# The gate product of layer 0 by seven half-width products

## The chip, the cores and the metric

The kernel runs on one core of a Trainium2 chip. The metric is the device time of one execution in microseconds (us). The core has five engines with instruction streams of their own: PE (matrix products, with weight loads listed apart as PEld), DVE and ACT (elementwise work), POOL and SP, which here mostly issue transfers. Sixteen DMA engines move the data of all queues.

## The reference

Two layers act on 256 tokens x and 256 context tokens, each with 2048 features. Every layer normalises, scales and shifts its input by a modulation computed from a condition vector, widens it to 4096 features, and projects it back. Layer 0 is a Fourier branch, layer 1 is attention with a window, context keys and a sink. The change is in layer 0:

```
u, z = split(h @ w_in, 2)            # h: 2048 features, u and z: 4096
f = real(fft2(u in 16 groups)) mixed per group by w_mix
y = f * silu(z)                      # the gate
x = x + gate * (y @ w_out)
```

The same is done with the context tokens, which have their own modulation but share the weights. So z is one product of 2048 x 4096 weights with 512 columns: 256 tokens and 256 context tokens. The modulation of layer 1 and the gate of layer 0 are products of a vector with 2048 x 2048 matrices (`adw`).

## The kernel before, in words

All products are made in parts: a value is split into a high part (`h`, rounded to fp32r by ACT, L60) and a low part (`l`, the rest, by DVE, L61), and `mm3` (L73 to L75) adds high x high, high x low and low x high in PSUM. `half_split` does that for half a raw weight tile (128 x 1024) into a pool of six buffers, that is three pairs; `raw` loads a 1 MB weight tile on SP's queue into one of three buffers.

The stages, in order of time on the page: the modulation of layer 0 and a transform along the tokens (to 120 us); the spectral stage, which computes f group by group (120 to 330 us) with matmuls of 256 and 260 columns and stores f to device memory (`fd`, L514); the gate stage (330 to 690 us, L558 to L618); the output product of layer 0 in two sweeps of 16 steps (to about 1030 us, L643 to L665); the key and value projection of layer 1 (`wkv`, to about 1123 us, L733 to L744), with the rope of the keys after it (L755); attention with the query and gate projections of layer 1 between its steps; the last output product.

In the spectral stage `fold_uh` makes sums and differences of weight halves. Some sums are made by a transfer on POOL's queue that adds its source to the tile it writes (L133, 508 bytes per run).

The gate stage first makes the 16 modulated input tiles `hs` (`make_hs`, L566: two operations on DVE and one on ACT per half, the input brought by POOL's queue). Each tile has 256 token columns and 256 context columns, as a high and a low part; together they fill 32 of the 34 buffers of the pool `act`. Four blocks of 128 output features are computed together while the inputs arrive, and then 28 blocks one by one: two weight halves are split, 16 x 3 matmuls of 512 columns run, `z_out` (L580) applies silu on ACT and multiplies by f on DVE (L584). f waits in 32 resident tiles `y`, loaded from `fd` by SP.

The generator `ada_jobs` (L530) does the remaining modulation as side work for DVE: 64 jobs, each a 1 MB weight tile and eight dot products of 512 columns (L545; the last 16 jobs four). One job is taken per block of the gate stage, 36 in the output stage by `ada_rate`. In the output stage the resident `y` are split again in each of the two sweeps (`y_split0`, L624).

The order of instructions on each engine comes from a scheduler that runs at build time: it takes program order as priority and what it simulates as ready. `tc.issue_after` adds an edge that holds the order by hand. Buffers of a pool are reused when all readers are done.

Of the kernel before, what the change touches and what calls it, by code (L numbers as in the profile page):

```python
# [10 lines left out]
F32 = mybir.dt.float32  # L11
F32R = mybir.dt.float32r
# [4 lines left out]
P = 128  # L17
# [4 lines left out]
N = 256  # L22
# [6 lines left out]
def tile_dit(ctx: ExitStack, tc: tile.TileContext, a: dict, out: bass.AP):  # L29
# [13 lines left out]
    def raw(src, q=None):  # L43
        t = rawp.tile([P, D], F32, tag="raw", name="raw")
        n = src.shape[-1]
        last_dma[0] = (q or nc.sync).dma_start(t[:, :n], src).ins
        return t

# [101 lines left out]
    r_bc = adap.tile([P, 512], F32, name="r_bc")  # L150

# [281 lines left out]


# [86 lines left out]
    def ada_done(i):  # L521
        layer, which, dst = ((0, 2, gt0), (1, 1, gs1), (1, 0, sh1), (1, 2, gt1))[i]
        ns = dst.shape[-1]
        V.tensor_tensor(acc[:, i, 0:2, :, 0:ns], acc[:, i, 0:2, :, 0:ns], acc[:, i, 2:4, :, 0:ns], op=ALU.add)
        V.tensor_tensor(dst, acc[:, i, 0, :, 0:ns], acc[:, i, 1, :, 0:ns], op=ALU.add)
        V.tensor_tensor(dst, dst, adab[:, layer, which, :, 0:ns], op=ALU.add)
        if (layer, which) == (1, 1):
            V.scalar_tensor_tensor(dst, dst, 1.0, ng[:, 1], op0=ALU.add, op1=ALU.mult)

    def ada_jobs():  # L530
        for pieces in ((0,), (1, 2, 3)):
            for kh in range(2):
                cb = adap.tile([P, 2, 1024], F32, tag="cb", name="cb")
                with tc.issue_after(hs_end[2]):
                    nc.gpsimd.dma_start(cb, a["crow"][:, kh].broadcast_to([P, 2, 1024]))
                with tc.issue_after(hs_end[1]):
                    S.activation(cb, cb, AF.Silu)  # L537
                for i in pieces:
                    for fg in range(8):
                        w = raw(a["adw"][i, kh, fg])  # L540
                        for f in range(2):
                            for kq in range(2):
                                wf = w[:, f * 1024 + kq * 512 : f * 1024 + kq * 512 + 512]
                                for s in range(2 if i < 3 else 1):
                                    V.tensor_tensor_reduce(junk if s == 0 and i < 3 else wf, wf, cb[:, s, kq * 512 : kq * 512 + 512], 1.0, 0.0, ALU.mult, ALU.add, acc[:, i, kh * 2 + kq, fg * 2 + f, s : s + 1])  # L545
# [11 lines left out]
    acc = adat.tile([P, 4, 4, KT, 2], F32, name="acc")  # L557
    with tc.tile_pool(name="yp", reuse_waits="tile", bufs=32) as ypool:  # L558
        ys = []
        for b in range(NB):  # L560
            y = ypool.tile([P, 512], F32, tag="y", name="y")
            ys.append(y)
        hs = []
        hs_end = [None] * 3

        def make_hs(k):  # L566
            xt = act()
# [9 lines left out]
            hs.append((h, l))  # L577

        with tc.tile_pool(name="zp", reuse_waits="tile", bufs=2) as zp:
            def z_out(b, o):  # L580
                y = ys[b]
                z = zp.tile([P, 512], F32, tag="z", name="z")
                S.activation(z, o, AF.Silu)
                V.tensor_tensor(y, y, z, op=ALU.mult)  # L584
                if b >= 4:
                    with tc.issue_after(hs_end[0]) if b < 8 else nullcontext():
                        next(ada)

            o4 = [psum() for _ in range(4)]
            for kg in range(4):  # L590
                wr = raw(a["wz0"][kg])
                w = []
                for i in range(2):
                    make_hs(kg * 4 + i * 2)
                    with tc.issue_after(hs_end[0]) if kg else nullcontext(), tc.issue_after(hs_end[1]) if kg else nullcontext():
                        w.append(half_split(wr, i))
                    make_hs(kg * 4 + i * 2 + 1)
                for j in range(4):
                    k = kg * 4 + j
                    wh, wl = w[j // 2]  # L600
                    for b in range(4):
                        q = slice((j % 2) * 512 + b * P, (j % 2) * 512 + (b + 1) * P)
                        mm3(o4[b], wh[:, q], wl[:, q], hs[k][0], hs[k][1], k == 0, k == KT - 1)
            for b in range(4):
                with tc.issue_after(last_dma[0]):
                    nc.sync.dma_start(ys[b], fd[b])
            for b in range(4):
                z_out(b, o4[b])
            for b in range(4, NB):
                w = ws_split(raw(a["wz"][b - 4]))  # L610
                with tc.issue_after(last_dma[0]):
                    nc.sync.dma_start(ys[b], fd[b])
                o = psum()
                for k in range(KT):
                    wh, wl = w[k // 8]
                    q = slice((k % 8) * P, (k % 8 + 1) * P)
                    mm3(o, wh[:, q], wl[:, q], hs[k][0], hs[k][1], k == 0, k == KT - 1)
                z_out(b, o)  # L618


        x1, sqs = [], []
        yy = {}

        def y_split0(i):  # L624
            for j in range(2):
                h, l = act(F32R), act(F32R)
                split(h, l, ys[i % 16 * 2 + j])
                yy[i, j] = (h, l)

# [14 lines left out]
        ada_rate = {2: 2, 5: 2, 8: 2, 11: 2, 15: 0, 16: 0, 19: 2, 22: 2, 25: 2, 28: 2, 30: 0, 31: 0}  # L644
        y_split0(0)
        for i in range(32):
# [4 lines left out]
            if i < 31:  # L651
                y_split0(i + 1)
            if kg >= 12:
# [12 lines left out]


# [11 lines left out]
    o = psum()  # L679
    PE.transpose(o[0:KT, 0:P], gt1.rearrange("p k s -> p (k s)"), ident)  # L680
    gr = const.tile([KT, P], F32, name="gr")
    S.copy(gr, o[0:KT, 0:P])
    nc.gpsimd.dma_start(gated.rearrange("o (k p) -> (o k) p", p=P), gr)
# [32 lines left out]
    with tc.tile_pool(name="h1", reuse_waits="tile", bufs=16) as h1p:  # L716
# [3 lines left out]
        with tc.tile_pool(name="kvp", reuse_waits="tile", bufs=2) as kvp:  # L720
            hc1 = []
# [12 lines left out]
            for kg in range(8):  # L734
                w = ws_split(raw(a["wkv"][kg]))
                for j in range(2):
                    k = kg * 2 + j
                    wh, wl = w[j]
                    for tb in range(4):
                        h = (hx1, hc1)[tb // 2][k]  # L740
                        c = (tb % 2) * P
                        for kv in range(2):
                            q = slice(kv * 512, (kv + 1) * 512)
                            mm3(o[tb][kv], h[:, c : c + P], h[:, N + c : N + c + P], wh[:, q], wl[:, q], k == 0, k == KT - 1)  # L744
            kr = []
            for tb in range(4):
# [6 lines left out]
                t = kvp.tile([P, 512], F32, tag="kr", name="kr", bufs=4)  # L753
# [5 lines left out]
            for hp in range(4):  # L759
# [5 lines left out]
                kT.append(t)  # L765

# [444 lines left out]
```

## Time and profile before

| | |
|---|---|
| median of three runs | 1863.13 us (1860.94 to 1863.33) |
| the profiled execution | 1861.45 us |
| its span in the trace | 1859.1 us |
| granted TensorE clock, mean | 0.995 |
| gate stage, 380 to 690 us | DVE 242.0 us busy of 310, DMA share 0.59, 219 GB/s |
| transfers in all | 367 MB, 198 GB/s |

A row of a group has: line, engine, operation, what it writes and reads, shape, number | busy time in all, mean duration of one in ns | idle time of that engine before it and what ended the wait. Rows of stretches give busy time of PE, weight loads, DVE, ACT and POOL with the number of instructions, then the granted clock, the share of the DMA engines in use, and GB/s. A matmul's duration is longer than the distance of two starts, because matmuls are pipelined; the pace is read from the starts.

### The profile page before, as it was taken

What the parts mean: (1) busy time and instruction counts of PE and PEld (TensorE: products, weight loads), DVE (VectorE), ACT (ScalarE), POOL (GpSimd) and SP (SyncE); (2) the same over time, 40 slices, a digit from 0 to 9 for tenths busy, and PEclk for the clock granted to TensorE, in tenths of its full rate; (3) what the DMA queues carried; (4) which work ended last, traced back from release to release, by engine and by line L of the source; (5) the groups of instructions that cost most, each with busy time, mean ns of one, the idle gap of its engine ahead of it and who ended that gap; (6) DMA issues with size and microseconds to landing.
All of it is one profiled execution on the core that took longest, in us unless ns stands there. A gap on an engine that the chain in (4) does not pass through costs nothing.

```text
span 1859.1 us, 26469 instructions
## 1 busy us (share of the span) xinstructions
PE 1817.6 (98%) x9889; PEld 1549.3 (83%) x9889; DVE 1389.6 (75%) x2766; ACT 954.6 (51%) x1657; POOL 176.8 (10%) x189
## 2 busy tenths in 40 slices
PE   6899999999999999999999999999999999999997
PEld 4579999888888888888888787888888888887886
DVE  4669888786868788687974825888878878887455
ACT  5444444432222243224322624888888888896343
POOL 0011111100000000000000001111220220300001
PEclk9899999999999999999999999999999999999999
DMA  9999888666656647763675323333333333434543
GB/s 395 407 296 246 246 220 242 228 226 244 224 212 234 227 172 264 264 236 131 226 286 204 114 92 143 128 136 126 124 115 135 136 115 135 159 137 179 186 178 136
DMA packets 76127, 367.39 MB, mean 198 GB/s; under 512 B 23200, under 2 KB 23344, under 8 KB 40928
## 3 DMA queue, kind: packets, MB, share of 16 engines
q1 hardware_dynamic: 49104, 324.83, 47.3%
q0 software_dynamic: 22320, 33.15, 7.1%
q10 hardware_dynamic: 4576, 7.74, 1.3%
q8 instruction: 77, 1.26, 0.3%
q14 instruction: 50, 0.41, 0.1%
HBM read 353.10 MB, written 12.59 MB: 197 GB/s over the span
## 4 chain that ended last, share of the span: by engine, by line
PE 90%; DMA 4%; DVE 3%; ACT 2%; issue 1%; POOL 0%; ACTq 0%; POOLq 0%; SPq 0%; DVEq 0%
PE ps L74 23%; PE ps L73 23%; PE ps L75 23%; PE ps L910 6%; PE ps L912 3%; DMA raw<-in_awp 3%; PE ps L966 3%; PE ps L981 2%; PE ps L980 2%; PE ps L946 2%; PE ps L947 2%; DMA raw<-in_wu 1%; PE ps L208 1%; PE ps L829 0%; DVE wl L61 0%
## 5 line engine op out<-in xcount | busy, mean ns | idle before, releaser
L60 ACT CAST wh<-raw 128x1024 fp32r<-128x1024 f32 x333 | 349.5, 1051 | 556.3 <-PE ps L74 483.5
L61 DVE TENSOR_TENSOR wl<-raw,wh 128x1024 fp32r<-128x1024 f32 x333 | 421.7, 1269 | 263.0 <-ACT wh L60 260.6
L74 PE MATMUL ps<-act,wh 128*128 128x512 f32 x1024 | 398.2, 389 | 0.0
L73 PE MATMUL ps<-act,wh 128*128 128x512 f32 x1024 | 393.6, 389 | 0.0
L75 PE MATMUL ps<-act,wl 128*128 128x512 f32 x1024 | 391.2, 389 | 0.0
L75 PEld LDWEIGHTS ps<-act,wl 128*128 128x128 f32 x1024 | 192.2, 188 | 39.9
L74 PEld LDWEIGHTS ps<-act,wh 128*128 128x128 f32 x1024 | 192.2, 188 | 39.8
L73 PEld LDWEIGHTS ps<-act,wh 128*128 128x128 f32 x1024 | 192.2, 188 | 39.8
L910 PE MATMUL ps<-h,wh 128*128 128x512 f32 x512 | 186.7, 400 | 0.0
L545 DVE CUSTOM_DVE_ANT_0 raw<-raw,cb 128x512 f32<-128x512 f32 x256 | 172.8, 689 | 14.5 <-DMA raw<-in_adw 10.6
L545 DVE CUSTOM_DVE_ANT_0 junk<-raw,cb 128x512 f32<-128x512 f32 x192 | 132.0, 687 | 10.8 <-ACT cb L537 8.3
L912 PE MATMUL ps<-h,wl 128*128 128x256 f32 x512 | 138.1, 280 | 0.0
L74 PE MATMUL ps<-wl,h 128*128 128x512 f32 x320 | 125.6, 392 | 1.5 <-DVE wl L61 1.5
L73 PE MATMUL ps<-wh,h 128*128 128x512 f32 x320 | 124.3, 397 | 0.2 <-ACT h L729 0.2
L75 PE MATMUL ps<-wh,h 128*128 128x512 f32 x320 | 124.4, 391 | 0.0
L910 PEld LDWEIGHTS ps<-h,wh 128*128 128x128 f32 x512 | 96.1, 188 | 18.7
L948 DVE CUSTOM_DVE_ANT_0 ps<-ps,mask,nsink 128x512 f32<-128x512 f32 x128 | 92.1, 754 | 11.8 <-PE ps L947 10.8
L951 ACT ACTIVATE p<-ps,mx 128x512 f32<-128x512 f32 x128 | 87.3, 687 | 24.6 <-DVE mx L948 24.0
L912 PEld LDWEIGHTS ps<-h,wl 128*128 128x128 f32 x512 | 96.8, 189 | 1.4
L61 DVE TENSOR_TENSOR pl<-ps,ph 128x512 fp32r<-128x512 f32 x128 | 83.7, 685 | 9.9 <-ACT ph L60 8.9
L956 ACT ACTIVATE p<-p,sm 128x512 f32<-128x512 f32 x128 | 85.4, 716 | 7.8 <-DVE sm L954 7.8
L74 PE MATMUL ps<-wl,ys 128*128 128x512 f32 x212 | 83.3, 393 | 0.0
(311 smaller groups left out, 3572.7 us busy)
## 6 DMA issues: line engine op xcount, KB each, us to landing
raw<-in_wz SPq DMA_DIRECT2D x64, 1024.0 KB, 4.9
raw<-in_adw SPq DMA_DIRECT2D x64, 1024.0 KB, 4.9
raw<-in_awp SPq DMA_DIRECT2D x32, 1024.0 KB, 13.8
raw<-in_wo SPq DMA_DIRECT2D x32, 1024.0 KB, 5.9
raw<-in_wq SPq DMA_DIRECT2D x32, 1024.0 KB, 4.8
raw<-in_wu SPq DMA_DIRECT2D x32, 1016.0 KB, 7.3
raw<-in_wo1b SPq DMA_DIRECT2D x16, 1024.0 KB, 4.9
act<-in_xT POOLq DMA_DIRECT2D x32, 256.0 KB, 5.6
```

The lines of the kernel that those rows point to most:

```text
L60: S.copy(h, src)
L61: V.tensor_tensor(l, src, h.bitcast(F32), op=ALU.subtract)
L73: PE.matmul(o, wh, xh, start=start, stop=False)
L74: PE.matmul(o, wh, xl, start=False, stop=False)
L75: return PE.matmul(o, wl, xh, start=False, stop=stop).ins
L545: V.tensor_tensor_reduce(junk if s == 0 and i < 3 else wf, wf, cb[:, s, kq * 512 : kq * 512 + 512], 1.0, 0.0, ALU.mult, ALU.add, acc[:, i, ...
L910: PE.matmul(o[0], wh[:, q], hx1[k], start=k == 0, stop=k == KT - 1)
L912: PE.matmul(o[0][:, 0:N], wl[:, q], hx1[k][:, 0:N], start=False, stop=False)
L948: V.tensor_tensor_reduce(o, o, mask[:, tb, :], -0.125, nsink[:, i : i + 1], ALU.add, ALU.min, mx[:, tb : tb + 1])
L951: S.activation(pt[:, tb, :], so[tb], AF.Exp, bias=mx[:, tb : tb + 1], scale=-1.0, accum_out=sm[:, tb : tb + 1])
L956: S.activation(pt[:, tb, :], pt[:, tb, :], AF.Copy, scale=sm[:, tb : tb + 1])
L966: PE.transpose(o[:, (kt * 2 + tb) * P : (kt * 2 + tb + 1) * P], pt[:, tb, c : c + P], ident)
```

## The change

For 13 pairs of blocks (26 of 32) the product is made by Strassen's scheme. The two blocks of weights and the two halves of their 2048 rows form a 2 x 2 matrix of weights, the tokens and the context columns, each cut in the same halves, the other. Instead of eight products of a weight quarter (1024 rows by 128) with 256 columns there are seven, of sums of weights with sums of inputs.

- Weights: per pair two tiles `r` and `q` (128 x 1024 each) and two tiles `rx` are loaded by SP. The sums are made in `r` and `q` by four accumulating transfers on POOL's queue, three of them issued after the split of the previous content.
- Inputs: the differences and sums of inputs are made once, by `make_t` and `make_t3`, in buffers of a new pool of 32.
- The units of the pairs are interleaved by a written table of slots, so that a sum has time to arrive. At the start and the end of the table the order is closer.
- The results of a unit are added from PSUM into tiles of z, then silu and the multiplication by f.
- f is loaded per block, y is stored to device memory (`yd`) by POOL and loaded again in the output stage. There the high and low parts are stored too (`yhl`) and the second sweep loads them instead of splitting again.
- Side work: in the gate stage a job is cut into four quarters, four quarters per pair and only for the first ten pairs, through buffers of `act`. In the output stage a dot has 1024 columns. The last 16 jobs (the gate of layer 1) move to the key and value projection as `gate_job`, two per step. The transpose of `gt1` moves with them.
- `issue_after` now holds the order of the weight loads on SP's queue until the end of the output stage.

The core of the diff:

```diff
+        for p in range(13):
+            for nm, t in (("5", 0), ("1", 1), ("2", 3), ("6", 5), ("7", 9), ("3", 11), ("4", 13)):
+                if p == 0:
+                    t = {"1": -2, "2": -1}.get(nm, t)
+                if p == 13 - 1:
+                    t = {"2": 10, "4": 11, "3": 12}.get(nm, t)
+                seq.append((7 * p + t, p, nm))
+        seq.sort()
...
+        def load_pair(p):
...
+            load(r, wz(b + 1, 0))
+            load(q, wz(b, 0))
+            nc.gpsimd.dma_start(out=r, in_=wz(b + 1, 1), accum_op=ALU.add)
...
+        def prep(n):
...
+            ready[n] = half_split(src, 0)
+            if nm in "561":
+                nc.gpsimd.dma_start(out=src, in_=wz(d["b"] + (nm == "1"), int(nm == "6")), accum_op=ALU.add)
...
+        def unit(n):
...
+            o = psum()[:, 0:N]
+            with tc.issue_after(zend[0]):
+                for k in range(K2):
+                    q = slice(k * P, (k + 1) * P)
+                    r = mm3(o, wh[:, q], wl[:, q], *tok[nm](k), k == 0, k == K2 - 1)
...
+            if nm == "7":
+                add(zc[:, lo], o, zb[:, hi])
+                add(zc[:, hi], d["n5"], zc[:, lo])
+                add(zb[:, hi], d["n5"], zb[:, hi])
+                S.activation(zc[:, hi], zc[:, hi], AF.Silu, scale=-1.0)
...
+            if 0 <= n + 2 < len(seq):
+                prep(n + 2)
+            if n >= 0:
+                unit(n)
+                if seq[n][2] in "5673" and seq[n][1] < 10:
+                    next(ada)
...
+        def make_t(k):
+            x, y = rt[k], rt.pop(k + K2)
+            x0, x1_, y0, y1_ = x[:, 0:N], x[:, N : 2 * N], y[:, 0:N], y[:, N : 2 * N]
+            V.scalar_tensor_tensor(x0, x0, dsh[:, 0, k : k + 1], x1_, op0=ALU.add, op1=ALU.subtract)
...
+                for q in range(2):
+                    nc.gpsimd.dma_start(yhl[i * 2 + j][q], (h, l)[q])
...
             for kg in range(8):
                 w = ws_split(raw(a["wkv"][kg]))
+                for i in range(2):
+                    gate_job(kg * 2 + i)
```

More of the change, by code (lines that the diff above doesn't have):

```diff
@@ new lines, in tile_dit @@
+        for k in range(K2):
+            make_t3(k)
+        seq = []
+        for p in range(13):
[6 more added lines that the diff above has]
+        seq.sort()
+        first = {}
+        for n, (_, p, nm) in enumerate(seq):
+            first.setdefault(p, n)
@@ L735, in tile_dit @@
                 w = ws_split(raw(a["wkv"][kg]))
+                for i in range(2):
+                    gate_job(kg * 2 + i)
                 for j in range(2):
```

297 lines of the change are left out of this document (225 added, 72 removed).

## The prediction

> **What bounds the kernel now.** I read the busy shares first, then the chain that ended last, then a table of stretches, and in the stretch that changes the rows of each engine.
>
> ```profile
> PE 1817.6 (98%) x9889; PEld 1549.3 (83%) x9889; DVE 1389.6 (75%) x2766; ACT 954.6 (51%) x1657; POOL 176.8 (10%) x189
> PE 90%; DMA 4%; DVE 3%; ACT 2%; issue 1%; POOL 0%; ACTq 0%; POOLq 0%; SPq 0%; DVEq 0%
> ```
>
> ```profile
> 120.00:320.00 200.00, 199.76 (x1654) 199.05 (x1653) 176.25 (x265) 97.36 (x187) 34.96 (x41) 1.00 0.88 237
> 380.00:690.00 310.00, 310.00 (x1369) 256.68 (x1369) 242.04 (x560) 88.96 (x108) 1.06 (x2) 1.00 0.59 219
> 690.00:1030.00 340.00, 340.00 (x1502) 281.53 (x1501) 260.89 (x599) 101.27 (x125) 10.71 (x20) 1.00 0.60 225
> ```
>
> Columns: stretch, length, busy PE, weight loads, DVE, ACT, POOL, then granted clock, DMA share, GB/s. The gate stage (380 to 690) is PE without a gap at full clock, so its time is matmuls times pace. The spectral stage (120 to 320) has the narrow matmuls and the accumulating transfers that the change brings to the gate stage: its DMA share is 0.88 at nearly the same GB/s as 0.59 below it. The paces come from the timeline of PE, start times in the first column:
>
> ```profile
> 274.18 0.28 PE L73 MATMUL ps<-act,wmh 128*127 128x256 f32 x1
> ...
> 279.17 0.28 PE L73 MATMUL ps<-act,wmh 128*127 128x256 f32 x1
> ```
> ```profile
> 499.74 0.39 PE L73 MATMUL ps<-act,wh 128*128 128x512 f32 x1
> ...
> 502.46 0.39 PE L73 MATMUL ps<-act,wh 128*128 128x512 f32 x1
> ```
>
> Between the first two lie 42 matmuls: 4.99/42 = 0.1188 us for 256 columns. Between the last two 12: 2.72/12 = 0.2267 us for 512. A half-width matmul costs 52.4% of a full one, not 50%.
>
> **The product itself.** A pair of blocks is now 2 x 16 x 3 = 96 matmuls of 512: 96 x 0.2267 = 21.76 us. Seven half products are 7 x 8 x 3 = 168 of 256: 168 x 0.1188 = 19.96 us (one unit: 2.85). That saves 1.80 us per pair, 13 x 1.80 = **23.4 us**, if PE stays the bound. The six first blocks keep full-width products. [...]
>
> **DVE in the gate stage.** Rows of 385 to 685 us:
>
> ```profile
> L545 DVE CUSTOM_DVE_ANT_0 raw<-raw,cb 128x512 f32<-128x512 f32 x112 | 77.2, 690 | 2.3
> L61 DVE TENSOR_TENSOR wl<-raw,wh 128x1024 fp32r<-128x1024 f32 x55 | 67.3, 1223 | 55.3 <-ACT wh L60 55.3
> ```
>
> Per pair, after: 7 splits x 1.22 = 8.5; 7 half-width adds from PSUM at 0.417 (L509's row) = 2.9; 2 multiplies x 0.686 = 1.4; four quarter jobs of the modulation, 8 x (0.689 + 0.083) = 6.2. Sum 19.0, against 2 x (2.45 + 0.69 + 6.18) = 18.6 now. Durations overlap: 233.2 us are busy in 385 to 685, where 27.5 blocks of 9.3 would sum to 256, a factor 0.91. So 17.3 of 19.96 us, 87% (now 78%). The last three pairs have no modulation. ACT has 7 x 1.05 + 1.7 = 9.1 us. Weight splits are prepared two units ahead over three buffers, so a split may be 5.7 - 2.3 = 3.4 us late before PE sees it. I cost DVE at nothing here; without that cover it is a rival.
>
> **DMA in the gate stage.** No row shows an accumulating packet of 4 KB. By the packets of the trace grouped by size: plain 2048 B take 84 ns, 4096 B 159, 8192 B 309, 512 B 25; accumulating 508 B (L133) take 65. Per pair, in engine time over 16 engines: four plain halves of weights 4 x 128 x 159/16 = 5.1; y in and out 4 x 0.67 = 2.7; four quarter loads 2.7; sum 10.5 us. An accumulating half lies between 128 x (159 + 39)/16 = 1.6 us (the extra of the 508 B row is fixed) and 128 x 65 x 4096/508/16 = 4.2 us (it grows with bytes). I take bytes moved twice plus the rest of that row, 2 x 159 + 15 = 333 ns, 2.7 us, because the same size's plain row is the nearer of the two in bytes. Four of them make 10.7, in all 21.1 us. Packet times overlap: at the eleventh accumulate of the spectral stage 11.06 us of packets went through in 10.13, so 21.1/1.09 = 19.4 of 19.96 us. DMA is nearly full, not yet the bound, and the latency has room: the sum for product 6 has five units, 14.3 us, and L133 landed in 6.7 to 13.5 us. [...]
>
> **The first units.** The order of the first pair is compressed to 1, 2, 5, 6, so product 6 follows 5 directly, while its weights need 5's split, then an accumulate into the same tile. Split of 5 starts when the last full block ends (its buffer is freed there): +2.3, landing +7 (L133: 6.7 to 13.5), split of 6 +2.3, together 11.6 us; units 1, 2 and 5 cover 8.6. Stall 3 us; bounds 1 (a 4 KB form landing faster) to 9. I take **4**. Ahead of it DVE has 16 x 1.6 (make_hs at the 0.395 us steps of L728 to L730), 12 + 3 splits, 8 make_t of about 2.5, six multiplies and eight make_t3: some 69 us, against 71 us of PE from 332.6 us (192 + 96 matmuls, two units). That is full, so a wait somewhere shows: **2**, bounds 0 to 8.
>
> **Entry.** Most input tiles move from the act pool to a pool that lies on memory of the spectral stage. Its first load now (L606) is issued at 331.49, the inputs at 323.5 to 329.4. PE starts block group 0 at 332.56 and uses an input per 2.7 us; two remain in act. The third is wanted at 338 and can be there at about 337. POOL's queue issues in order and the inputs wait there behind the last stores. I take **2**, bounds 0 to 6.
>
> **The output stage and after.** The branch goes to device memory and back: DMA per step 2.5 weights, 2.6 modulation, 1.0 in, 2.7 hi and lo out, 8.9 of 10.9 us; the second sweep 2.5 + 3.2 + 2.7. DVE falls (1024-wide dots, no second split). PE was unbroken at DMA share 0.60; I cost it at 0, bounds -1 to 5. The key/value projection (1040 to 1123 us) gets 16 gate jobs, 32 dots. DVE is busy 30.93 + 11.03 = 42 us there; a 1024-wide dot is bounded by 0.69 and 2 x 0.69, with its reading about 1.22: 39 us, together 81 of 83. The rope of the keys (1123.57) is queued behind the last dots and q's splits behind that. **2**, bounds 0 to 8. Raw buffers now pass through slow dots there, so weights of the next step can be late too. The dropped transpose of gt1 was beside other work: 0.
>
> **Sum.** -23.4 + 4 + 2 + 2 + 2 = -13.4. The profiled execution's 1861.45 us (span 1859.1 and 2.35 around it) gives 1848.1; that execution lies 1.7 below the median of 1863.13, so 1849.8 there. I predict 1850 as median; a change within 0.2% (3.7 us) of 1863 cannot be told from none.
>
> **Rivals.**
> - *Accumulates fill the DMA engines* (slower). Place: the thirteen pairs. If cost grows with bytes, four take 16.8, in all 27.2/1.09 = 24.9 us per pair, 22.5 without modulation: 10 x 3.2 + 3 x 0.7 = +34 against now, plus 4 at the ends: about 1900. DMA is the bound from a packet of 352 ns on (10.5 + 4 x 128 x 0.352/16 = 21.8 = 19.96 x 1.09). At 400 ns a pair takes 23.3/1.09 = 21.4: ten times 0.36 and three times 1.8 saved, 9 us, against tolls of 10, so that is where it turns. For it: the share of 0.88 in the spectral stage. Against: most of that is 508 B packets. 0.25, spread over 1867 to 1905.
> - *DVE becomes the bound* while modulation runs. A unit 7 slot has 1.2 + 1.25 + 1.55 = 4.0 us of DVE in 2.85; if order and waits for ACT cost 0.3 us per split and add, 10 x 14 x 0.3 less the free 10 x 2.6 gives +16: 1866, or some 1862 where such waits fall together with the tolls above. Against: splits have 3.4 us of room. 0.10, counted as same.
> - *DMA half full*: packets near 370 to 390 ns eat most of the gain: 1859 to 1866. 0.07, same.
> - *The half pace does not hold* because contiguous 128-column weights load slower than 127: the ml/mh rows at 272.6 to 273.5 are 128 wide and also 0.12 apart. 0.02, slower.
> - *Forecast*: PE stays the bound, 1838 to 1859. 0.56.
>
> Faster 0.56, same 0.17, slower 0.27. The range 1838 to 1885 leaves out the upper part of the first rival and little below.
>
> **What would show it.** PE's starts 0.119 us apart in the units and 19.9 to 20.5 us from one product 5 to the next; a stall near 3 us ahead of the first product 6; accumulating packets near 330 ns; DMA share in the pairs near 0.95; DVE near 0.87. Wrong: idle PE with ACT's cast waiting for a DMA of weights (first rival), or for DVE (second). If PE is unbroken in the pairs but the end is no earlier, the time went to the key/value stage.

## The result and the profile after

The changed kernel takes **1947.67 us** (median of four runs, 1946.87 to 1958.51) where the kernel before took 1863.23 in the same session: ratio 1.0463, interval 1.042 to 1.0505. It is 84 us slower, where a gain of 13 us had been predicted. Its profiled execution is the slowest of the four, 1958.51 us with a span of 1956.7, so stage lengths below add up to 97.6 us against the span of before. All stage lengths in this document come from one profiled execution of each kernel, while times and ratios are medians; the two need not move by the same amount.

The page's first row and its chain, for the changed kernel:

```profile
PE 1833.3 (94%) x10825; PEld 1593.9 (81%) x10825; DVE 1450.1 (74%) x2553; ACT 993.2 (51%) x1716; POOL 309.3 (16%) x404
PE 35%; ACT 1%; issue 1%; DVE 0%; ACTq 0%; POOLq 0%; POOL 0%
```

PE has fallen from 98 to 94%. The chain, followed back from the end, covers only 37% of the span here, so it says nothing of the stages that changed. The table of stretches does (stretch, length, busy PE, weight loads, DVE, ACT, POOL, granted clock, DMA share, GB/s); cut at the first six blocks, which keep the full product, the pairs, the step to the output stage, and its two sweeps:

```profile
343.00:422.00 79.00, 67.69 (x284) 54.48 (x283) 63.28 (x132) 38.49 (x73) 12.81 (x22) 0.94 0.52 180
422.00:734.00 312.00, 276.38 (x2182) 270.83 (x2181) 206.10 (x370) 116.38 (x147) 61.79 (x84) 0.96 0.95 254
734.00:744.00 10.00, 0.82 (x4) 0.60 (x3) 4.25 (x7) 4.21 (x7) 3.21 (x6) 0.64 1.09 376
744.00:922.00 178.00, 176.08 (x769) 144.90 (x768) 138.76 (x206) 50.41 (x62) 49.91 (x94) 0.99 1.05 382
922.00:1113.00 191.00, 182.42 (x770) 145.77 (x769) 152.79 (x242) 40.50 (x45) 23.06 (x44) 0.98 0.77 275
```

In none of them is PE whole, where before it was from 332 to 1032 us, and the clock has fallen below 1.00. DVE in the pairs is busy for 66%, not 87%: it waits. Stage lengths, from the starts of the first matmuls of each stage:

| us | before | after | difference |
|---|---|---|---|
| start to first gate matmul | 332.6 | 339.3 | +6.7 |
| first six blocks (288 full matmuls) | 66.5 | 82.3 | +15.8 |
| other 26 blocks | 282.9 | 312.4 | +29.5 |
| step to the output stage | – | 9.5 | +9.5 |
| output stage | 348.2 | 369.5 | +21.3 |
| from there to the end | 829.0 | 843.7 | +14.7 |

Of the change, little more than two small subtractions on DVE lies ahead of the first gate matmul. Over the variants below, which are edited behind it, it starts between 330.9 and 343.6 us, so the first row can't be put down to the change.

**How one stall comes about.** The waits of 420 to 700 us in the changed kernel (engine, tile and line that waited, what it waited for: us in all, times, longest):

```profile
DVE junk L539 <- DMA act<-in_adw: 65.6, 31, 4.8
ACT wh L63 <- DMA raw<-in_wz: 43.9, 10, 18.6
PEld ps L78 <- DVE wl L64: 31.9, 23, 4.9
PE ps L78 <- DVE wl L64: 26.9, 20, 4.7
```

PE waits for the low half of weights (`wl`), whose split on DVE is late; and DVE itself stands for 65.6 us before a dot product of the side work (`junk`) whose tile has not landed. The timeline of DVE around one such stall:

```profile
597.51 1.22 DVE L64 TENSOR_TENSOR wl<-raw,wh 128x1024 fp32r<-128x1024 f32 x1
602.18 0.69 DVE L539 CUSTOM_DVE_ANT_0 junk<-act,cb 128x512 f32<-128x512 f32 x1 [3.46 <-DMA act<-in_adw]
...
604.72 0.69 DVE L539 CUSTOM_DVE_ANT_0 junk<-act,cb 128x512 f32<-128x512 f32 x1 [0.90 <-DMA act<-in_adw]
605.34 0.08 DVE L539 DVE_READ_ACCUMULATOR2_ANT acc<- 128x1 f32 x1
605.34 1.22 DVE L64 TENSOR_TENSOR wl<-raw,wh 128x1024 fp32r<-128x1024 f32 x1
```

and that of PE beside it:

```profile
604.52 0.28 PE L77 MATMUL ps<-t,wh 128*128 128x256 f32 x1
606.62 0.38 PE L78 MATMUL ps<-t,wl 128*128 128x256 f32 x1 [1.81 <-DVE wl L64]
...
607.21 0.42 PE L76 MATMUL ps<-t,wh 128*128 128x256 f32 x1
607.43 0.42 PE L77 MATMUL ps<-t,wh 128*128 128x256 f32 x1
...
610.61 0.28 PE L77 MATMUL ps<-t,wh 128*128 128x256 f32 x1
610.73 0.28 PE L78 MATMUL ps<-t,wl 128*128 128x256 f32 x1
```

Two dots wait for loads; the split that PE needs is queued behind the second and ends at 606.56; PE starts at 606.62. Then from 607.2 to 610.6 starts are 0.21 us apart instead of 0.119: the granted clock is half for 3.4 us. Why the tiles came late is seen in SP's timeline, and in the time from issue to landing of the two loads that the dots waited for (issued in 587 to 588.5 and in 594 to 596 us):

```profile
587.44 7.63 SPq L588 DMA_DIRECT2D act<-in_adw  x2
597.62 0.33 SPq L588 DMA_DIRECT2D rx<-in_wz  x1
```
```profile
act<-in_adw SPq DMA_DIRECT2D x1, 256.0 KB, 14.7
act<-in_adw SPq DMA_DIRECT2D x1, 256.0 KB, 10.0
```

The first load was issued at 587.44 and took 14.7 us to land, at a DMA share of about 1.0. The second was issued only at 594.74, when an earlier dot had freed a buffer of `act`, of which two are left over, and took 10.0 us. So both count: slow landing and a queue that stands. Between 420 and 700 us that queue stood for 138.7 us behind dots (28 times), with weights and f queued behind.

### The profile page after: what moved, and what is told of

It is laid out like the page before. It is cut to its first block, busy times and chain, and to the rows that moved or that the text cites. A ratio compares the mean times of both kernels' runs of the same rounds, so it can differ in the third digit from the quotient of the medians.

```text
span 1956.7 us, 28956 instructions
## 1 busy us (share of the span) xinstructions
PE 1833.3 (94%) x10825; PEld 1593.9 (81%) x10825; DVE 1450.1 (74%) x2553; ACT 993.2 (51%) x1716; POOL 309.3 (16%) x404
## 3 DMA queue, kind: packets, MB, share of 16 engines
q1 hardware_dynamic: 61776, 333.23, 46.6%
## 5 line engine op out<-in xcount | busy, mean ns | idle before, releaser
L64 DVE TENSOR_TENSOR wl<-raw,wh 128x1024 fp32r<-128x1024 f32 x346 | 435.5, 1264 | 177.3 <-ACT wh L63 168.6
L76 PE MATMUL ps<-act,wh 128*128 128x256 f32 (+1 forms) x768 | 251.3, 335 | 20.2 <-ACT wh L63 19.2
L77 PE MATMUL ps<-act,wh 128*128 128x256 f32 (+1 forms) x768 | 255.3, 335 | 2.7 <-DVE act L603 2.7
L78 PE MATMUL ps<-act,wl 128*128 128x256 f32 (+1 forms) x768 | 232.3, 335 | 6.1 <-DVE wl L64 6.1
L76 PEld LDWEIGHTS ps<-act,wh 128*128 128x128 f32 x768 | 147.0, 191 | 36.4 <-ACT wh L63 21.1
L78 PEld LDWEIGHTS ps<-act,wl 128*128 128x128 f32 x768 | 146.7, 191 | 22.2 <-DVE wl L64 8.3
L77 PEld LDWEIGHTS ps<-act,wh 128*128 128x128 f32 x768 | 147.2, 192 | 17.2 <-DVE act L603 3.1
L539 DVE CUSTOM_DVE_ANT_0 raw<-raw,cb 128x1024 f32<-128x1024 f32 x108 | 130.9, 1222 | 7.2 <-DMA raw<-in_adw 3.4
L539 DVE CUSTOM_DVE_ANT_0 junkw<-raw,cb 128x1024 f32<-128x1024 f32 x76 | 92.7, 1220 | 40.7 <-ACT cb L548 23.6
L78 PE MATMUL ps<-t,wl 128*128 128x256 f32 x312 | 93.9, 301 | 21.1 <-DVE wl L64 20.9
L76 PE MATMUL ps<-yr,wh 128*128 128x512 f32 x256 | 103.4, 404 | 8.6 <-ACT wh L63 8.6
L77 PE MATMUL ps<-yr,wh 128*128 128x512 f32 x256 | 102.1, 399 | 0.0
L76 PE MATMUL ps<-t,wh 128*128 128x256 f32 x312 | 92.3, 296 | 7.9 <-ACT wh L63 7.9
```

Of the source, the lines that this page charges most:

```text
L64: V.tensor_tensor(l, src, h.bitcast(F32), op=ALU.subtract)
L76: PE.matmul(o, wh, xh, start=start, stop=False)
L77: PE.matmul(o, wh, xl, start=False, stop=False)
L78: return PE.matmul(o, wl, xh, start=False, stop=stop).ins
L539: V.tensor_tensor_reduce(o, x, y, 1.0, 0.0, ALU.mult, ALU.add, dst)
```

## The experiments

Theories: **full DMA**, called A below (the accumulating transfers bring the engines to their limit, and that sets the pace), against **side work**, called B (its late loads stand in DVE's order ahead of the weight splits; and after the pairs, the side work that was displaced there costs). The first four texts add C: DVE has too much to do. Later texts use the letters for the rivals that they name. Times are medians, ratios are against the kernel before.

### The pairs: four kernels that each take one thing away

s1 leaves the jobs of the gate stage out; s2 keeps their loads and drops the dots; s3 keeps the dots on a resident tile and drops the loads; s4 keeps both and lets the weight transfers overwrite instead of accumulate:

```diff
# s1: none of these lines; s2: without the two of dot; s3: without w and load, dot reads cb
-                                w = act()
-                                load(w, src[:, j * 512 : (j + 1) * 512])
-                                for s in range(2):
-                                    dot(w if s else junk, w, cb[:, s, kq * 512 : kq * 512 + 512], acc[:, i, kh * 2 + kq, fg * 2 + f, s : s + 1])
# s4, both sums
-            nc.gpsimd.dma_start(out=r, in_=wz(b + 1, 1), accum_op=ALU.add)
+            nc.gpsimd.dma_start(out=r, in_=wz(b + 1, 1))
```

> The ten modulation jobs of the gate stage are left out, loads and dot products (their sums stay zero); all else is the changed kernel. Measured is the time from the first to the last half-width matmul, 312.4 us in the changed kernel against 259.5 of bare matmul pace. Theory A (the DMA engines are full): 2.7 us of packets per pair go, about 17 of 20 us remain, so 265 to 285 us. Theory B (queues held by one another: SP's queue waits for a buffer of the side work, DVE stands in front of a side load that lands late, weight splits stand behind it): the same 265 to 285 us. Theory C (DVE has too much to do): the same. The run gives the size of what the side work costs, about 30 to 45 us, in whichever way.

> The side loads of the gate stage stay, their dot products are left out, so nothing on DVE waits for them and their buffers come free at once. Bytes are those of the changed kernel. Theory A: the pairs stay at 300 us or more. Theory B: 265 to 285 us. Theory C: 265 to 285 us.

> The dot products of the side work stay in number and size but read a resident tile (the condition vector itself, so the modulation is another), and their loads are left out. Theory A: bytes fall by 2.7 us of packets per pair, 265 to 285 us. Theory B: no late load in front of DVE and no held SP queue, 265 to 285 us. Theory C: DVE is as busy as in the changed kernel, 300 us or more.

> The accumulating transfers overwrite instead of adding (the weight sums are replaced by the last summand); count, bytes and places stay. A packet of 4 KB should fall from 326 ns to about 159, 5.3 us of packets per pair. Theory A: the pairs fall to 265 to 285 us. Theory B: they fall by the shorter landing of sums and side loads alone, to 290 to 305 us. Theory C: unchanged, 305 us or more.

| | time | ratio | pairs, us | seven units, us (pairs 3 to 10) |
|---|---|---|---|---|
| after | 1947.67 | 1.0463 | 312.4 | 23.47 |
| s1, no side work | 1925.24 | 1.0341 | 275.6 | 20.05 |
| s2, loads only | 1919.27 | 1.0308 | 285.5 | 20.58 |
| s3, dots only | 1926.81 | 1.0349 | 276.7 | 20.05 |
| s4, plain sums | 1911.07 | 1.0264 | 274.3 | 20.06 |

The stretch of 470 to 560 us in the changed kernel, then in s2, s3 and s4:

```profile
470.00:560.00 90.00, 80.75 (x657) 78.71 (x656) 62.77 (x119) 32.85 (x42) 17.44 (x23) 1.00 0.99 268
```
```profile
470.00:560.00 90.00, 89.66 (x751) 89.46 (x750) 55.20 (x71) 39.43 (x50) 19.18 (x25) 1.00 1.04 299
```
```profile
470.00:560.00 90.00, 90.00 (x756) 90.00 (x756) 76.63 (x141) 41.41 (x50) 22.39 (x30) 1.00 1.02 269
```
```profile
470.00:560.00 90.00, 90.00 (x756) 90.00 (x755) 75.55 (x145) 39.96 (x49) 14.99 (x28) 1.00 0.90 314
```

s2 moves more bytes per second than the changed kernel (299 against 268 GB/s) at a DMA share of 1.04 and loses 0.5 us per seven units against s1, 10 us over all the pairs (285.5 against 275.6): full DMA engines cost something, but they don't set the pace of the changed kernel. s3 and s4 do all the dots in an unbroken pace: nor does DVE. The large cost comes only of loads and dots together: a late load, a dot that waits for it, and a split behind the dot. s1 and s3 lie in the range of side work, s2 is half a microsecond above it where full DMA asked 300 or more, and s3 rules out C, which asked as much.

s4 missed its expectation: 274.3 us lies in the range of full DMA (265 to 285), not in that of side work (290 to 305). So the accumulating packets do matter, and side work and full DMA are no clean rivals. With plain sums side loads land in 7.2 us as a median (9.2 in the changed kernel, both 470 to 650 us), and the wait of DVE for them over 450 to 690 us falls from 59.4 to 15.0 us:

```profile
DVE junk L539 <- DMA act<-in_adw: 15.0, 19, 1.7
```

The medians of the whole move less than the pairs do: in s1 the pairs are 36.8 us shorter and the time is 22.4 us shorter.

### The lead of the side load

If a late load in front of DVE is the cause, an earlier load must mend it. s6 issues it one quarter job ahead, s9 three quarter jobs ahead with four buffers (two free constants' tiles beside two of `act`). Both compute everything.

```diff
# s6
-                                for s in range(2):
-                                    dot(w if s else junk, w, cb[:, s, kq * 512 : kq * 512 + 512], acc[:, i, kh * 2 + kq, fg * 2 + f, s : s + 1])
+                                side_dots()
+                                side.append((w, cb, kq, i, kh, fg, f))
...
# s9
-                                w = act()
+                                w = act() if j % 2 == 0 else c32.rearrange("p k s -> p (k s)") if j == 1 else r_bc
...
+                                if len(side) == 3:
+                                    side_dots()
+                                side.append((w, cb, kq, i, kh, fg, f))
```

> Each side load of the gate stage is issued one job before its dot products, so that DVE should find it landed; bytes and dots are those of the changed kernel. Time from first to last half-width matmul (312.4 in the changed kernel, 275 to 277 without either half of the side work). Theory B (DVE waits in order for side loads, and splits behind it come late): 270 to 290 us. Theory A (bytes set the pace, the three runs before only lightened them): 305 us or more, since no byte is saved.

> The side loads of the gate stage go round four buffers instead of two (two of act and two tiles that are dead by then) and stand three quarter jobs ahead of their dots. Bytes, dots and their number are those of the changed kernel. Units take 312.4 us in the changed kernel, 308.3 with a lead of one, 285.5 with the same bytes and no dots. Theory B, narrowed (loads on SP's queue stand behind a side load that waits for its buffer, and DVE in front of a side load that landed late; a lead of one did not help as two buffers made the load wait all the same): 275 to 292 us. Theory A (bytes set the pace): 303 us or more.

s6: 1952.56 us (1.0476), pairs 308.3, DVE's wait over 450 to 690 us still 56.6 us. The theory as stated for this run fell: with two buffers the load ahead holds the one that the next load needs, and nothing is earlier. s9: 1929.49 us (1.0337), pairs 292.7, seven units 21.58. Its stretch beside that of the changed kernel above has six microseconds more of PE:

```profile
470.00:560.00 90.00, 87.03 (x706) 85.94 (x705) 68.12 (x130) 36.89 (x47) 18.27 (x24) 0.98 1.02 284
```

So the lead brings back 20 of the 37 us that leaving the side work out does (312.4 to 292.7, against 275.6), with all work done. It is a little short of what the theory asked (275 to 292). More buffers weren't tried, nor an order on DVE with the splits ahead of the dots.

### The order of the loads

At 734.02 PE stops for 9.5 us. SP's timeline, then ACT's, of the changed kernel:

```profile
729.56 2.21 SPq L588 DMA_DIRECT2D y<-yd  x4
731.87 0.90 SPq L47 DMA_DIRECT2D raw<-in_wo  x1
```
```profile
742.38 1.04 ACT L63 CAST wh<-raw 128x1024 fp32r<-128x1024 f32 x1 [3.00 <-DMA raw<-in_wo]
```

The first output weights are issued behind four loads of y, which wait until the last y are stored and buffers come free. In the same way the weights of the last full block waited behind loads of f (40 us, a stop of 8.0 us at 400.55; stops are given from one start of a matmul to the next). s7 issues both sets of weights, and those of the first two pairs, ahead, and moves product 6 of the first pair two units later; s11 is s7 without side work in the pairs, and with two early output weights instead of one; s8 leaves out the gate jobs beside the keys and values.

```diff
+        full = [raw(a["wz"][b - 4]) for b in range(4, NB - 2 * 13)]
+        for p in range(2):
+            load_pair(p)
...
-                    t = {"1": -2, "2": -1}.get(nm, t)
+                    t = {"1": -2, "2": -1, "6": 8.5, "3": 12.5}.get(nm, t)
...
-            for p in range(13):
+            for p in range(2, 13):
...
+        wo_first = raw(a["wo0"][0, 0])
```

> Three edits of order alone: the weights of the last full block and of the first two pairs are loaded ahead of the loads of f that wait for buffers; product 6 of the first pair stands two units later and 3 one later; the first weights of the output stage are loaded ahead of the y loads that wait for buffers. Theory of held queues: the stall of 8 us in the last full block goes, that of 6 to 11 us ahead of the first product 6 goes, and the 9.5 us ahead of the output stage fall to 1 or 2; 20 to 25 us of the total in all. Theory A (bytes): the stalls return a little later, as the same bytes have to pass: under 8 us.

> The edits of order (with the first two weight tiles of the output stage ahead of the y loads) and no side work in the pairs: what the product can give when nothing else is in its stage. By theory B and A alike 259.5 us of bare pace and the rest of the first stalls: units 262 to 268 us, idle time ahead of the output stage under 2 us, total 1900 to 1912. That the total still stands above 1863 would say that the moved work, not the product, costs the rest.

> The sixteen gate jobs of the key and value projection are left out, loads and dots (the gate of layer 1 is its bias alone). Time from the end of the output stage to the end of the trace, 843.7 us in the changed kernel against 829 in the kernel before. If the jobs crowd DVE and the raw buffers there (the prediction's term of 2 us, bounds 0 to 8, was too small): 829 to 833 us. If the excess comes from elsewhere, such as the clock after the gaps at the start: 838 us or more.

s7: 1931.93 us (1.0365). The six full blocks take 78.0 us instead of 82.3, the pairs 298.6, the step 0.1. But a stop of 9.65 us stands one step further on, at 722.11 (the second output weights, behind the same loads of y), and the output stage takes 374.3. The whole gains 16 us: less than the 20 to 25 that held queues asked and more than the 8 of full DMA, and a stall did return later, as full DMA had it. s11: 1907.3 us (1.0218), pairs 268.3, but 378.2 in the output stage: even so, some 41 us slower than the kernel before beside it. s8: 1945.26 us (1.0437); the stretch after the output stage is 838.4, so 5.3 of its 14.7 us come from the gate jobs and most from elsewhere.

### The output stage

s5 drops the round trip of the high and low parts and splits y again, as before; s10 leaves out the side work of the second sweep (layer 1's shift and scale lack it).

```diff
# s5
-                for q in range(2):
-                    nc.gpsimd.dma_start(yhl[i * 2 + j][q], (h, l)[q])
...
-            if i < 15:
+            if i < 31:
                 y_split0(i + 1)
# s10
-            for _ in range(ada_rate.get(i, 1)):
+            for _ in range(ada_rate.get(i, 1) if i < 16 else 0):
```

> The high and low parts of y are neither stored to device memory nor loaded: y stays in its 28 tiles (the first two pairs are loaded once more) and the second sweep splits again, as in the kernel before. Measured: first to last matmul of the output stage, 369.5 us in the changed kernel against 348.2 of bare pace, and the idle time ahead of it (9.5). Theory A2 (the round trip fills the DMA engines: 33 MB more, a share of 1.05 in the first sweep): 350 to 356 us. Theory B2 (SP's queue is held in order by the side work's raw buffers and by slow dots, bytes matter little): 362 us or more. The idle time ahead stays near 9.5 by both.

> The 21 modulation jobs of the second sweep of the output stage are left out (layer 1's scale and shift are zero). The second sweep takes 191 us in the changed kernel against 174.1 of bare pace. If the side work moved there from the gate stage and its 1 MB loads in three raw buffers hold the weights up: 174 to 177 us for that sweep, the first unchanged near 178. If the loads of y's parts on POOL's queue hold it up: 183 us or more.

s5: 1965.6 us (1.0546), with sweeps of 179.8 and 192.5 us at DMA shares of 0.68 and 0.65, where the changed kernel has 178.4 and 191.1 at about 1.05 and 0.79. In the first sweep both kernels split alike, and fewer bytes gain nothing: bytes are not what it suffers from. In the second the splits are back on DVE (151.8 us busy of 190 in the changed kernel, 166.9 in s5), so for that sweep s5 is no clean test. s10: 1945.22 us (1.0421); the second sweep falls from 191.1 to 179.2. Its bare length is 174.1, so 12 of 17 us are the side work, between what the two theories asked. The median time falls by only 2.4 us: in s10's profiled execution the first sweep and the stretch after the output stage are 2.3 and 3.5 us longer than in the changed kernel's.

### Together, and each alone

s12 joins s9 and s7 and computes everything. x13 is the kernel before, unchanged in its product, with only the side work placed as in the change (ten jobs in the gate stage, 1,024-wide dots in the output stage, gate jobs beside keys and values, and the tiles and the transpose that move with them). x14 is s7 with no side work at all, and with two early output weights, as in s11.

```diff
# x13, against the kernel before
-                if b >= 4:
+                if b >= 6 and b % 2 == 0 and b < 26:
                     next(ada)
...
+        ada_rate = {5: 2, 10: 2, 15: 0, 16: 0, 30: 0, 31: 0, **{i: 2 for i in (17, 19, 20, 22, 24, 25, 27, 28)}}
...
+                for i in range(2):
+                    gate_job(kg * 2 + i)
# x14, against s7: no load and no dots, and
-            for _ in range(ada_rate.get(i, 1)):
+            for _ in range(0):
```

> Side loads on four buffers three ahead, and all edits of order; nothing is left out, the result is the reference's. By theory B the gains of both add: 270 to 280 us of units, no idle time ahead of the output stage, total 1900 to 1915. By theory A: 1930 or more, as with the order alone (1931.9). Neither would reach the kernel before.

> The kernel before, with its gate product as it was (32 full blocks), and only the side work placed as in the change: ten jobs in the gate stage, the others in the output stage as dot products 1,024 wide, and the sixteen of layer 1's gate beside the keys and values. Everything is still computed. Theory A (what the change lost outside the pairs comes from the displaced side work): the second sweep of the output stage takes 183 us or more where the kernel before took 174.1, the stretch from the output stage's end to the kernel's end 835 us or more where it took 829.0, and the time is 1,875 to 1,890. Theory B (it comes from what the change's own new structure leaves behind: buffers, the load queue held in order, late weights): both sweeps stay within 176 us, the rest within 832, and the time is 1,860 to 1,870.

> The change with its weights issued early (the order edits of s7) and with all the side work left out, in the gate stage, the output stage and beside the keys and values (sums of the modulation are left out of the computation; the gate of layer 0 and the shift and scale of layer 1 then lack them). Theory A (displaced side work is what costs outside the pairs): units 262 to 270, the output stage 348 to 356 us, the rest 829 to 835, and the time 1,840 to 1,868. Theory B (the new structure itself): the output stage stays at 362 us or more or the rest at 840 or more, and the time is 1,880 or more.

| us | before | s12 | x13 | x14 |
|---|---|---|---|---|
| time | 1863.5 to 1865.9 | 1920.13 | 1910.64 | 1876.56 |
| ratio, interval | 1 | 1.0275, 1.0247 to 1.0302 | 1.0248, 1.0201 to 1.0295 | 1.0066, 1.0042 to 1.0091 |
| first six blocks | 66.5 | 79.6 | 66.5 | 80.5 |
| other blocks | 282.9 | 287.1 | 282.9 | 269.2 |
| output stage | 348.2 | 374.5 | 368.5 | 353.3 |
| after it | 829.0 | 843.2 | 853.4 | 837.5 |

s12 is the best version of the change that computes everything, and still 2.75% slower than the kernel before. Its pairs (287.1) and its time are above what side work asked (270 to 280, 1900 to 1915), and the time is below the 1930 of full DMA.

**x13 settles most.** With the old product, whose gate stage stays whole (351.57 of 352 us), the new places of the side work alone cost 47 us, more than the theory asked: the second sweep takes 194.5 us, where it took 174.1, and the stretch after the output stage 853.4. Stretches of x13 (second sweep, then the step to the keys and values with their product) and, in the second fence, of the kernel before:

```profile
857.00:1035.00 178.00, 165.50 (x697) 134.88 (x697) 158.41 (x251) 53.44 (x69) 6.95 (x13) 0.96 0.62 224
1035.00:1200.00 165.00, 145.03 (x629) 118.51 (x628) 113.87 (x203) 59.82 (x95) 8.15 (x7) 0.92 0.58 209
```
```profile
855.00:1030.00 175.00, 175.00 (x774) 144.91 (x773) 134.50 (x304) 56.26 (x73) 5.89 (x11) 1.00 0.57 214
1030.00:1200.00 170.00, 165.37 (x802) 138.04 (x800) 103.88 (x182) 89.69 (x155) 16.39 (x14) 0.99 0.36 126
```

The rows of DVE's dots say why: first x13 over 857 to 1060 us, then the kernel before over 855 to 1030 us.

```profile
L532 DVE CUSTOM_DVE_ANT_0 raw<-raw,cb 128x1024 f32<-128x1024 f32 x48 | 58.3, 1219 | 3.1 <-DMA raw<-in_adw 2.5
L532 DVE CUSTOM_DVE_ANT_0 junkw<-raw,cb 128x1024 f32<-128x1024 f32 x41 | 49.9, 1218 | 0.8 <-DMA raw<-in_adw 0.8
```
```profile
L545 DVE CUSTOM_DVE_ANT_0 raw<-raw,cb 128x512 f32<-128x512 f32 x66 | 43.6, 690 | 8.5 <-DMA raw<-in_adw 8.0
L545 DVE CUSTOM_DVE_ANT_0 junk<-raw,cb 128x512 f32<-128x512 f32 x33 | 22.8, 691 | 0.0
```

Dots took 66.4 us of the second sweep; now 108.2 fall there and just behind it. A 1,024-wide dot is cheaper than two of 512 (1.22 + 0.08 against 2 x 0.77 us), but before, 17 jobs are taken in that sweep and eight of them have only four dots (the sixteen such jobs come as two groups of eight, the first of them in the first sweep), while now it is 21, all of full width. And side loads and weights pass through the same three raw buffers, in one queue: it stood behind dots for 90.5 us over 857 to 1060 us, and in the kernel before for 43.7 over 857 to 1030. SP's timeline in x13, then ACT's, then PE's:

```profile
903.37 6.16 SPq L46 DMA_DIRECT2D raw<-in_adw  x2
910.95 0.33 SPq L46 DMA_DIRECT2D raw<-in_wo  x1
```
```profile
920.27 1.04 ACT L60 CAST wh<-raw 128x1024 fp32r<-128x1024 f32 x1 [7.11 <-DMA raw<-in_wo]
```
```profile
921.37 0.79 PE L73 MATMUL ps<-act,wh 128*128 128x512 f32 x1 [3.42 <-ACT wh L60]
```

The weights are issued only when the dots have freed a buffer, land too late, and PE stops. After the sweep the last sums of squares (L653) stand behind dots too: PE waits 8.8 us for them and 6.5 us for the norm's root, at half clock for 20.5 us from 1064.8 on (mean granted clock 0.92 over 1035 to 1200 us).

**x14 is the rest.** Without any side work (its stretches of the pairs and the output stage):

```profile
414.00:684.00 270.00, 263.90 (x2189) 262.96 (x2188) 166.94 (x214) 118.50 (x150) 59.09 (x79) 0.99 0.97 256
684.00:1037.00 353.00, 353.00 (x1537) 288.06 (x1536) 116.03 (x140) 90.91 (x108) 75.76 (x144) 1.00 0.68 227
```

The step from s7 to x14 is 55 us (1931.93 to 1876.56), the side work but for one more early output weight: 25 of it come with the jobs of the gate stage (to s11) and 31 with those after it. It lies between the two theories' ranges, since something of the new structure remains: 13 us above the kernel before, although that one does all the side work. By stages, against before: six full blocks +14.0, pairs -13.7, output stage +5.1, after it +8.5.

### The slower second sweep

In x14 the output stage's PE has no gap, yet the matmuls of the second sweep are 0.2333 us apart, those of the first 0.2267: 5.1 us. The tiles come from another pool and by a transfer. Where the second sweep multiplies tiles of `act` that were split there, as in x13 and in the kernel before, its unbroken parts keep 0.227. Two kernels move the tiles of x14:

```diff
-        wide[0] = yl.tile([P, 1024], F32, name="junkw", bufs=1)
+        wide[0] = yl.tile([P, 1032], F32, name="junkw", bufs=1)[:, 0:1024]   # x16: 1280
```

> The kernel of x14 (no side work anywhere, so layer 0's gate and layer 1's shift and scale lack it), with the tiles that the second sweep of the output stage multiplies moved by 32 bytes. In x14 that sweep took 0.2333 us per matmul without a gap and at full clock, where the first sweep took 0.2267: 5.1 us in 768 matmuls. Theory A (where the tiles lie sets that pace): it changes, to 0.2267 or to another value. Theory B (it comes from the transfers that write the tiles or from the values): it stays 0.2333.

> The same with the tiles moved by 1,024 bytes (and the same parts left out). Theory A: the pace of the second sweep changes here or in the run with 32 bytes. Theory B: 0.2333 in both.

Measured, in one execution each: 1876.45 and 1878.22 us, paces 0.2342 and 0.2333. A small shift hardly matters, so that theory fell as it was put; whether it is the region of memory or the values' way there stays open. It explains s10's 179.2 us: 174.1 and 5.1 of this.

## Why the prediction was wrong, point by point

- **The product** (-23.4): right. Seven units without disturbance took 20.05 us (s1, s3), predicted 19.96, before 21.76: 13 x 1.71 = 22 us.
- **The accumulating packet** (333 ns, between 198 and 524): right. Most take 326 ns, plain ones of the same size 159. Half a megabyte of them lands in 10.3 us as a median (470 to 650 us), within the 14.3 us of room.
- **"DMA is nearly full, not yet the bound", and "I cost DVE at nothing here"**: this step failed, though both halves are true by themselves (DMA share 0.99 to 1.02 with PE unbroken in s3 and s11, 470 to 650 us; DVE 75.55/4.5 = 16.8 us per pair in s4, predicted 17.3). Loads landed late in the changed kernel: at a DMA share of 0.99 a quarter load took 9.2 us as a median (470 to 650 us), up to 15.3, where s4 at 0.91 had 7.2. The prediction weighed throughput and gave the latency only of accumulates, though plain packets in the accumulates' place take the loss away (s4). It named the cover of DVE, 3.4 us per split, but didn't set what uses it up against it: a dot of the side work in DVE's order, with a load that has two buffers. Steady pairs lost 3.4 us for every seven units (23.47 against 20.05), the whole gain and more. By the signs that the prediction named, PE waited 26.9 us for DVE's half of a split and 8.4 for ACT's cast (420 to 700 us).
- **The first units** (+4, bounds 1 to 9): mechanism right, size wrong, and one stop not counted. Units 0 to 6 took 40.4 us against 20, with stops of 4.95 and 8.31 us and 17 us of half clock around them. The second stop is the one predicted, ahead of product 6; the sum landed in 11.5 us, not in 7. The first, in product 5, is its split behind a dot of the side work that waits 4.76 us for its load; in s1 it is gone, and the units take 35.1. Two units more for the sum, weights issued earlier and no side work (s11) leave 27.7.
- **Entry and the new input tiles** (+2 and +2): mechanism right, too small: +15.8 in the first six blocks. The longest stop, 8.0 us, was a load that no step counted, the last full block's weights behind f loads in SP's queue. With these weights ahead, 11.5 us stay in s7 and 14.0 in x14, where matmuls wait for late input tiles (PE stops of 3.4 and 4.5 us in x14).
- **The step to the output stage**: not in the sum. 9.5 us, weights behind loads of y that wait for the last stores.
- **The output stage** (0, bounds -1 to 5): wrong. "DVE falls (1024-wide dots, no second split)" was false: in the two sweeps DVE is busy for 138.76 + 152.79 = 291.6 us, before for 268.9 (684 to 1032 us), and most of the rise is in the second (134.5 of 175 us before, 152.79 of 191 after). With rows it had (0.77 us a dot) the prediction could have counted the second sweep: 99 dots of 512 that run in it before, 76 us; 21 full jobs after, 84 dots of 1,024, 102 us at its own estimate of 1.22. That was left out, and the price of a raw buffer held by dots stands only in a half sentence on the next stage.
- **Keys and values** (+2, bounds 0 to 8): +14.7. Gate jobs are 5 to 6 of it (s8, x14). 8.5 stay without them, 5.2 of these between the keys' transposes and the first scores (46.6 us against 41.4); their tiles and a transpose were moved there. x13, with the same moves and the old product, has 48.4 us there, so the new product is not needed for it; the moves weren't tried alone, and which of them it is stays open.
- **Rivals**: the first, "accumulates fill the DMA engines", gave about 1900, the nearest number, but not its cause: its price began at 352 ns a packet, measured are 326, and s2 runs at full DMA with 10 us lost in the pairs. That its number came near is luck. The second, DVE as the bound, named order and waits with 0.3 us per split; that was nearer to the mechanism, and far too small. No rival had the price of the side work, the largest item: 55 us by s7 and x14, of which 25 go with the jobs left in the gate stage and 31 with those behind it; displaced alone, in the old kernel, it is 47 (x13). The loads' order is 16 (after to s7), and 13 stay from the rest of the new structure when the gain of the product is taken off: together the 84. No term of the sum was for half clock behind stops either; by the estimate in the last section some 25 us, spread over these items.

## What to carry to other kernels

The busy share of an engine decided nothing by itself here: over 470 to 560 us DVE was busy for 85% in s3, with PE unbroken, and for 70% in the changed kernel, where PE stood for 9 us. Look for what stands in an engine's order with an input that can be late, and count buffers for that input at the latency that the changed stage has (here 9.2 us for a quarter load at a DMA share of 0.99, 7.2 at 0.91 in s4). Work that is displaced has a price at its new place (47 us in x13); count it there per stretch (here per sweep), with the buffers and the queue that it shares with what PE waits for. Where a kernel keeps side work hidden under a long stage, shortening that stage sends the work elsewhere, and moving the side work alone, in the kernel before (x13), is the experiment to make first.

## What the runs showed of the hardware

- **Half clock after short stops.** In the changed kernel the granted clock was 0.5 behind idle time of PE, from 330 us on for 3.413 us or a multiple of it each time, but for a last stretch of 10.16 us up to the end of the trace. That makes 81.8 us (before: 11.6), some 50 of them with PE at work, so by estimate 25 us are lost this way. The stop of 1.81 us from 604.80 on was followed by 3.4 us of half clock, by estimate 1.7 us more: it cost about twice its length. The length of a stop alone didn't decide. In the changed kernel all such stretches begin a whole number of 3.413 us apart (at 443.31, 607.15, 658.35 and 682.24 us: 48, 15 and 7 steps). Of the steps on this grid in the gate and output stages, those in which PE was idle for 1.81 us or more were followed by half clock, those with 1.41, 1.44, 1.51 and 1.58 were not. So 1.82 us of idle time from 558.30 on, cut in two by the grid, cost no clock, and 1.81 us from 604.80 on, inside one step, did. Behind the output stage two steps with 1.47 us of idle time (from 1115.74 and from 1218.14 on) were followed by half clock too, so the trace gives no one length that decides.
- **An accumulating transfer** of 4 KB packets took 326 ns a packet in the changed kernel, 2.05 times a plain one (159).
- **The same matmul at two paces**: 0.2267 and 0.2333 us at full clock and without gaps, the second with inputs from another pool (x14, and over 930 to 980 us the changed kernel); two small shifts of the tiles changed it by 0.001 at most (x15, x16). The cause is open.
